# Two whole rows or four half rows: how the last block joins the column groups of TensorE

## The chip, the cores and the metric

The kernel runs on one core of a Trainium2 chip. A core has TensorE (matrix products, result in PSUM), VectorE, ScalarE, GpSimd and SyncE, each with its own list of instructions, and 16 DMA engines that bring data from HBM. The metric is the device time of one execution in microseconds.

## The reference, cut to what matters

```python
B, S, D = 8, 8192, 512                      # x: [B, S, D] fp32, w: [D, D] fp32
mask = (pos < lengths[:, None, None])       # lengths drawn per batch
cs = np.cumsum(x * mask, axis=1)
mid_features = cs[b_idx, lengths // 2, :]   # one row per batch
out = mid_features @ w                      # [8, 512]
```

Only one row of the running sum is used per batch. So what is computed is, for each batch, the sum of its first min(length // 2 + 1, length) rows of x, and then one product with w.

## The kernel before, in words

**Summing with TensorE.** Rows come in blocks of 512: 128 partitions with G = 4 rows each, so a tile of a block is [128, 4, 512]. A matmul with a [128, 8] matrix of ones and zeros as weights adds one of the four rows of all partitions (128 rows of x) to the sums of the 8 batches; the column of the batch that the block belongs to holds ones. A result of 8 rows needs only a quarter of TensorE's columns. The helper `add(j, weights, rows)` (L510 to 515) puts a matmul into column group j: its result stands in partitions 32j to 32j+7 of the PSUM tile s_ps ([128, 512]), and four matmuls with different j can run side by side. Row j of a block goes to group j. At the end the four groups hold four partial sums per batch.

In the profile each fp32 matmul is two records on TensorE (two passes) and two weight loads, which stand under PEld.

**Which blocks there are.** For the lengths drawn, the first full blocks of batches 0 and 1 are in tile first. Another 23 full blocks come through tile xt, in three slots of two blocks each. What is left of each batch, under 512 rows, comes through tile rem. The only full block of the last batch, batch 7, is in tile last: this is the "last block".

**Who issues what.** SyncE issues the transfers of first, xt and last (L188, L222, L255). ScalarE issues those of w and rem. The transfers of last are issued behind all others, in four parts named by ENDS (L63): rows 0 and 1 (512 KB), row 2 (256 KB), the first half of row 3 and its second half (128 KB each). Each part has a semaphore of its own, s_last[0] to s_last[3].

**TensorE's list.** After the first blocks comes a loop over rounds (L555): for each slot it adds up to two blocks and one batch's rest. The order behind the loop is written out by hand:
- L576 to 579: wait for the first part of last, then add its rows 0 and 1 to s_ps, row 0 in group 0 and row 1 in group 1.
- L580, `tell()` (L530): a 1x1 matmul whose end raises s_pe. VectorE waits for it (L496) before it copies s_ps.
- L581 to 586: wait for row 2 and for the first half of row 3, and add them to another PSUM tile, t_ps, with `add_columns(h, weights, row)` (L517). This helper takes half h of the 512 columns and gives 64 columns to each of the four groups. Rows 2 and 3 so bypass s_ps and its copy.
- L587 and 588: wait for VectorE's copy of the first 256 columns of s_ps into s_sb (L498), and fold the four groups' partial sums into t_ps, with a 0/1 matrix (fold) as weights.
- L589 to 593: wait for the second half of row 3, add it to t_ps; wait for the second copy, fold it.
- L594 to 603: the product of the transposed sums (t_sb) with w, 16 matmuls of 128 columns, four groups by four chunks.

**VectorE's list** at that point is two copies of s_ps (256 columns each), two transposes of t_ps into t_sb (L501), and two copies of one half of the result (L506). ScalarE copies the other half (L329). SyncE and ScalarE write one half each (L258, L332). All of VectorE's steps go through the helper `step` (L360).

Of the kernel before, what the change touches and what calls it, by code (L numbers as in the profile page):

```python
# [17 lines left out]
def kernel(  # L18
# [29 lines left out]
    B, S, D = x.shape  # L48
# [25 lines left out]
    def sb(name, shape, dt=F32):  # L74
        return ctx.enter_context(nc.sbuf_tensor(name, shape, dt))

    def ps(name, shape):
        return ctx.enter_context(nc.psum_tensor(name, shape, F32))
# [6 lines left out]
    last = sb("last", [P, G, D])  # L85
# [33 lines left out]
    e_last = sb("e_last", [P, B])  # L119
# [15 lines left out]
    s_ps = ps("s_ps", [P, D])  # L135
# [13 lines left out]
    def take(eng, s, n):  # L149

        eng.wait_ge(s, n).then_inc(s, -n)  # L151

    def pairs(eng, n, body, k=0, most=NS):

        if k < most:
            with eng.If_cmp(n, 2 * k + 1, "IS_GE"):
                body(k)
                pairs(eng, n, body, k + 1, most)

    def rounds_of(eng, n, least):  # L160

        assert all((i + PER - 1) * 43 >> 8 == -(-i // PER) for i in range(ITEMS))
        to = eng.alloc_register(f"{eng.engine.name}_rounds")
        eng.reg_alu(to, n, PER - 1, ALU.add)
        eng.reg_alu(to, to, 43, ALU.mult)
        eng.reg_alu(to, to, 8, ALU.logical_shift_right)
        eng.reg_alu(to, to, least, ALU.max)
        return eng.snap(to, min_val=least, max_val=ROUNDS)

    def less(eng, n, by):  # L170
        eng.reg_alu(n, n, by, ALU.subtract)
        eng.reg_alu(n, n, 0, ALU.max)
# [22 lines left out]
    @contextmanager  # L195
    def ending(eng, name, hint):

        eng.br(name)
        with nc.body(name, valid_engines=OrderedEngineSet([eng.engine])):
            yield  # L200
            eng.br(f"{name}_end").branch_hint(hint)
        nc.switch_bb(f"{name}_end")
# [305 lines left out]

    @block.tensor
    def _(pe):  # L510
        def add(j, weights, rows):

            return pe.matmul(s_ps[32 * j:32 * j + B], lhsT=weights, rhs=rows,  # L513
                             start=False, stop=False, skip_group_check=True,
                             tile_position=(0, 32 * j))

        def add_columns(h, weights, row):  # L517

            for j in range(4):
                at = D // 2 * h + P // 2 * j  # L520
                mm = pe.matmul(t_ps[h][32 * j:32 * j + B, :P // 2], lhsT=weights, rhs=row[:, at:at + P // 2],  # L521
                               start=False, stop=False, skip_group_check=True, tile_position=(0, 32 * j))
            return mm

        def keep_busy(n=1):

            for _ in range(n):
                pe.matmul(idle_ps[:], lhsT=idle[:], rhs=idle[:, :1].to_broadcast((P, D)), start=True, stop=True)  # L528

        def tell():  # L530

            pe.matmul(idle_ps[:1, :1], lhsT=tick[:], rhs=tick[:], start=True,  # L532
                      stop=True).then_inc(s_pe, 1)

        pe.addr_align(256, offset=80, max_nops=0)

        hint = pe.mark_branch_hint_location()
        pe.wait_ge(s_dve, DVE_SEL)
        pe.matmul(s_ps[:], lhsT=zero[:], rhs=zero[:, :1].to_broadcast((1, D)), start=True,  # L539
                  stop=False, skip_group_check=True)  # L540
        pe.wait_ge(s_dve, DVE_N)
        pe.matmul(n_ps[:, :B], lhsT=ones[:], rhs=len_f[:], start=True, stop=True).then_inc(s_pe, 1)  # L542
        pe.wait_ge(s_pool, 2)
        left, some, has_last = [pe.alloc_register(f"pe_{n}") for n in ("left", "some", "has")]
        pe.wait_ge(s_dve, DVE_FIRST)
        pe.load([has_last, left], addr[:, :2])
        pe.reg_mov(some, B)
        rounds = rounds_of(pe, left, RR)
        for b in range(BLIND):
            pe.wait_ge(s_first[b], 16)  # L550
            for j in range(G):
                add(j, cur_first[:, b], first[:, b, j])
        BUSY = [3, 1, 0]
        pe.wait_ge(s_dve, DVE_MASK)
        with pe.Fori(0, rounds):  # L555
            def add_pair(k):
                keep_busy(BUSY[k])
                take(pe, s_full[k], 32)
                with pe.If_cmp(left, 2 * k + 2, "IS_GE"):
                    for j in range(G):  # L560
                        add(j, cur[:, k, 1], xt[:, k, 1, j])
                for j in range(G):
                    mm = add(j, cur[:, k, 0], xt[:, k, 0, j])
                mm.then_inc(s_done[k], 1)

            for k in range(NS):
                pairs(pe, left, add_pair, k, k + 1)
                with pe.If_cmp(some, k + 1, "IS_GE"):
                    take(pe, s_rem[k], 16 * (len(PARTS) + 1))
                    for j in range(G):  # L570
                        mm = add(j, cur_rem[:, k, j * B:(j + 1) * B], rem[:, k, j])
                    mm.then_inc(s_rdone[k], 1)
            less(pe, left, PER)
            less(pe, some, NS)

        with pe.If_cmp(has_last, 1, "IS_GE"):  # L576
            pe.wait_ge(s_last[0], 16)
            for g in range(2):
                add(g, e_last[:], last[:, g])
        tell()  # L580
        with pe.If_cmp(has_last, 1, "IS_GE"):  # L581
            pe.wait_ge(s_last[1], 16)
            for h in range(2):
                add_columns(h, e_last[:], last[:, 2])
            pe.wait_ge(s_last[2], 16)
            add_columns(0, e_last[:], last[:, 3])
        pe.wait_ge(s_dve, DVE_ALL + 1)  # L587
        add_columns(0, fold[:], s_sb[:]).then_inc(s_pe, 1)
        with pe.If_cmp(has_last, 1, "IS_GE"):  # L589
            pe.wait_ge(s_last[3], 16)  # L590
            add_columns(1, e_last[:], last[:, 3])
        pe.wait_ge(s_dve, DVE_ALL + 2)
        add_columns(1, fold[:], s_sb[:]).then_inc(s_pe, 1)
        with ending(pe, "product", hint):  # L594
            pe.wait_ge(s_w, 32)
            for kc in range(KC):
                if kc % 2 == 0:
                    pe.wait_ge(s_dve, DVE_ALL + 3 + kc // 2)
                for j in range(4):
                    mm = pe.matmul(o_ps[32 * j:32 * j + B, :P], lhsT=t_sb[:, kc, :B],  # L600
                                   rhs=wt[:, kc, j * P:(j + 1) * P],
                                   start=(kc == 0), stop=(kc == KC - 1), tile_position=(0, 32 * j))
            mm.then_inc(s_pe, 1)
# [33 lines left out]
```

## Time and profile before

| What | us |
|---|---|
| Time, median of 5 executions | 84.63 (84.38 to 85.02) |
| Time of the profiled execution | 84.69 |
| its span, first to last instruction | 82.9 |
| TensorE busy (385 matmul records) | 56.8 |
| VectorE busy | 15.0 |
| ScalarE busy | 7.4 |
| Landing of the first part of last released TensorE at | 75.80 |
| VectorE's first copy of s_ps started at | 76.89 |
| The output's transfers were issued at | 79.95 and 80.01 |

The span is counted from the first instruction. The time is that of the whole execution, so 1.8 us lie around the span. A view in order of time gives start, length, engine, line, operation, output <- input, shape and number of records; in brackets stands how long the engine was idle before, and what released it. The ends of matmuls are modelled by the profiler, so starts are more telling than lengths: a record of 512 columns shows about 0.59 us, yet the next one in the same group starts 0.43 us after it. The clock granted to TensorE stands per slice in tenths of full speed.

### The profile page before, as it was taken

Reading aid. Unit: us, or ns where it says so; the run is one execution under the profiler, and the core shown is the slowest. Engines: PE = TensorE matmul, PEld = TensorE weight load, DVE = VectorE, ACT = ScalarE, POOL = GpSimd, SP = SyncE. Lnnn points to the kernel's source line nnn. Section 1 sums busy time; section 2 is a strip of 40 time slices with the busy share of each in tenths; the row PEclk is TensorE's granted clock in tenths of the full one; section 3 lists DMA queues with packets and bytes.
Section 4 is the critical chain, followed back from the end, with each engine's and each line's share of the span. In section 5 each row is a group of like instructions: output and inputs, shape, how many; then the busy total and the mean of one; then the engine's idle time right before and its main releaser. Section 6 shows DMA issues by size and latency. Waiting matters only on the chain. (4 is left out here: it accounts for less than half of the span.)

```text
span 82.9 us, 1505 instructions
## 1 busy us (share of the span) xinstructions
PE 56.8 (69%) x385; PEld 15.1 (18%) x385; DVE 15.0 (18%) x79; ACT 7.4 (9%) x8; POOL 1.3 (2%) x14
## 2 busy tenths in 40 slices
PE   2800799297075399999290199999988989188820
PEld 2300023021020112321110011321311411011510
DVE  2858897001001001001000000000000000000620
ACT  0999300000000000000000000000000000000020
POOL 5000000000000000000000000000000000000000
PEclk9999999999999957999999555899999999999999
DMA  0999999999999999999999999999999999997000
GB/s 20 380 419 429 453 427 416 406 419 411 451 435 427 419 387 423 419 407 427 423 427 419 434 432 412 466 411 419 443 411 459 419 411 443 391 400 276 0 1 14
DMA packets 3827, 31.26 MB, mean 377 GB/s; under 512 B 562, under 2 KB 834, under 8 KB 1618
## 3 DMA queue, kind: packets, MB, share of 16 engines
q1 hardware_dynamic: 2754, 27.27, 78.5%
q10 hardware_dynamic: 1072, 3.97, 12.1%
q8 instruction: 1, 0.02, 0.1%
HBM read 31.23 MB, written 0.02 MB: 377 GB/s over the span
## 5 line engine op out<-in xcount | busy, mean ns | idle before, releaser
L513 PE MATMUL s_ps<-xt,cur 128*8 128x512 f32 x184 | 25.0, 663 | 15.6 <-PEq L151 15.6
L528 PE MATMUL idle_ps<-idle 128*128 128x512 f32 x32 | 15.9, 620 | 0.0
L513 PEld LDWEIGHTS s_ps<-xt,cur 128*8 128x8 f32 x184 | 4.2, 92 | 33.7 <-issue 33.7
L477 DVE TENSOR_TENSOR cur<-since 128x16 f32 x9 | 1.7, 188 | 44.4 <-DVEq L151 44.4
L513 PE MATMUL s_ps<-rem,cur_rem 128*8 128x512 f32 x64 | 9.7, 680 | 0.0
L528 PEld LDWEIGHTS idle_ps<-idle 128*128 128x128 f32 x32 | 5.4, 190 | 12.5 <-issue 12.5
L329 ACT COPY o_sb<-o_ps 8x128 f32<-8x128 f32 x2 | 0.5, 259 | 70.4 <-PE o_ps L600 70.4
L513 PE MATMUL s_ps<-first,cur_first 128*8 128x512 f32 x16 | 3.3, 965 | 5.0 <-DVE since L360 5.0
L273 ACT ACTIVATE rem<-rem 128x2048 uint32<-128x2048 uint32 x3 | 5.5, 1892 | 0.0
L513 PEld LDWEIGHTS s_ps<-rem,cur_rem 128*8 128x8 f32 x64 | 2.1, 102 | 6.5 <-issue 6.5
L539 PE MATMUL s_ps<-zero 1*128 1x512 f32 x2 | 2.1, 1136 | 1.6 <-DVE zero L360 1.6
L360 DVE COPY s_sb<-s_ps 128x256 f32<-128x256 f32 x2 | 0.8, 424 | 12.0 <-PE idle_ps L532 11.9
L513 PEld LDWEIGHTS s_ps<-first,cur_first 128*8 128x8 f32 x16 | 0.4, 101 | 6.5 <-issue 5.1
L486 DVE COPY cur_rem<-table 128x32 f32 x5 | 0.9, 181 | 3.4 <-DVEq L151 3.4
L271 ACT ACT_TABLE_LOAD x1 | 1.3, 1283 | 1.9 <-issue 1.9
L600 PE MATMUL o_ps<-wt,t_sb 128*8 128x128 f32 x32 | 1.1, 273 | 0.1
L360 DVE TENSOR_TENSOR part_a<-since,step_a 1x42 f32<-1x42 f32 (+1 forms) x2 | 1.1, 562 | 0.1
L513 PE MATMUL s_ps<-last,e_last 128*8 128x512 f32 x4 | 1.0, 594 | 0.0
L521 PE MATMUL t_ps<-last,e_last 128*8 128x64 f32 x32 | 1.0, 220 | 0.0
L360 DVE TENSOR_TENSOR since<-item,begin 1x42 f32<-1x42 int32 (+1 forms) x2 | 0.8, 422 | 0.1
L600 PEld LDWEIGHTS o_ps<-wt,t_sb 128*8 128x8 f32 x32 | 0.8, 89 | 0.3 <-issue 0.3
L542 PEld LDWEIGHTS n_ps<-len_f,ones 1*128 1x128 f32 x2 | 0.7, 332 | 1.0 <-DVE above L360 0.5
(70 smaller groups left out, 14.2 us busy)
## 6 DMA issues: line engine op xcount, KB each, us to landing
xt<-in_x_dram SPq DMA_DIRECT2D x10, 2048.0 KB, 13.6
xt<-in_x_dram SPq DMA_DIRECT2D x3, 1024.0 KB, 10.9
first<-in_x_dram SPq DMA_DIRECT2D x2, 1024.0 KB, 7.5
rem<-in_x_dram ACTq DMA_DIRECT2D x3, 512.0 KB, 8.0
wt<-in_w_dram ACTq DMA_DIRECT2D x2, 512.0 KB, 5.6
rem<-in_x_dram ACTq DMA_DIRECT2D x3, 256.0 KB, 8.2
last<-in_x_dram SPq DMA_DIRECT2D x1, 512.0 KB, 7.6
rem<-in_x_dram ACTq DMA_DIRECT2D x3, 128.0 KB, 7.8
```

The lines of the kernel that those rows point to most:

```text
L271: act.memzero(lens1[:, 2 * B:])
L273: act.memzero(rem[:, q]).then_inc(s_rfree[q], 1)
L329: copy = act.copy(out=o_sb[1][:, j * P:(j + 1) * P], in_=o_ps[64 + 32 * j:64 + 32 * j + B, :P])
L360: do(*args, **kw).then_inc(s_dve, 1)
L477: dve.tensor_tensor(out=cur[:, k], in0=since[:, :B, here].rearrange("p b h -> p h b"), in1=since[:, 1:, here].rearrange("p b h -> p h b"), ...
L486: dve.tensor_copy(out=cur_rem[:, k], in_=rests[:, ds(dve.snap(of, min_val=1, max_val=RR - 1), 1), k].rearrange("p o w -> p (o w)"),).then_ ...
L513: return pe.matmul(s_ps[32 * j:32 * j + B], lhsT=weights, rhs=rows, start=False, stop=False, skip_group_check=True, tile_position=(0, 32 * j))
L521: mm = pe.matmul(t_ps[h][32 * j:32 * j + B, :P // 2], lhsT=weights, rhs=row[:, at:at + P // 2], start=False, stop=False, skip_group_check= ...
L528: pe.matmul(idle_ps[:], lhsT=idle[:], rhs=idle[:, :1].to_broadcast((P, D)), start=True, stop=True)
L539: pe.matmul(s_ps[:], lhsT=zero[:], rhs=zero[:, :1].to_broadcast((1, D)), start=True, stop=False, skip_group_check=True)
L542: pe.matmul(n_ps[:, :B], lhsT=ones[:], rhs=len_f[:], start=True, stop=True).then_inc(s_pe, 1)
L600: mm = pe.matmul(o_ps[32 * j:32 * j + B, :P], lhsT=t_sb[:, kc, :B], rhs=wt[:, kc, j * P:(j + 1) * P], start=(kc == 0), stop=(kc == KC - 1) ...
```

## The change

`add` takes a slice of columns, which applies to the result and to the moving operand alike. Behind the loop the first part of last is added by four matmuls of 256 columns where there were two of 512: row 0's left half in group 0 and its right half in group 1, row 1's left half in group 2 and its right half in group 3. The folds add all four groups, so it doesn't matter which group a piece of a row is in. All other calls of `add` keep their 512 columns.

```diff
-        def add(j, weights, rows):
-
-            return pe.matmul(s_ps[32 * j:32 * j + B], lhsT=weights, rhs=rows,
+        def add(j, weights, rows, columns=slice(0, D)):
+
+            return pe.matmul(s_ps[32 * j:32 * j + B, columns], lhsT=weights, rhs=rows[:, columns],
                              start=False, stop=False, skip_group_check=True,
                              tile_position=(0, 32 * j))
...
         with pe.If_cmp(has_last, 1, "IS_GE"):
             pe.wait_ge(s_last[0], 16)
-            for g in range(2):
-                add(g, e_last[:], last[:, g])
+            for j in range(4):
+                add(j, e_last[:], last[:, j // 2], slice(D // 2 * (j % 2), D // 2 * (j % 2 + 1)))
         tell()
```

On the engines' lists this is the only difference: two matmuls 8x512 become four of 8x256, and VectorE, ScalarE, GpSimd and SyncE have the same instructions in the same order.

## The prediction

> **What bounds the kernel.** I read the row of slices first, then the chain that ended last, then the tail in order of time.
>
> The slices show two regimes. The granted TensorE clock, the busy share of the DMA engines and the rate, over 40 slices of 2.07 us:
>
> ```profile
> PEclk9999999999999957999999555899999999999999
> DMA  0999999999999999999999999999999999997000
> GB/s 20 380 419 429 453 427 416 406 419 411 451 435 427 419 387 423 419 407 427 423 427 419 434 432 412 466 411 419 443 411 459 419 411 443 391 400 276 0 1 14
> ```
>
> From slice 1 to 35 the DMA engines are full at about 420 GB/s, whatever TensorE does. In slice 36 (74.6 to 76.7 us) they run dry, and what follows no transfer of x bounds. So the body is bound by memory, and the change, which touches no transfer, can only act behind the last landings. The chain that ended last covers just that tail (start us, length, what):
>
> ```profile
> 74.93 1.78 PE s_ps L513 x11
> 76.70 0.06 PE t_ps L521 x3
> 76.77 0.10 PE idle_ps L532
> 76.86 0.02 issue
> 76.89 0.43 DVE s_sb L360
> 77.32 0.02 issue
> 77.34 0.43 DVE s_sb L360
> ...
> 77.87 0.26 DVE t_sb L360
> 78.13 0.14 issue
> 78.27 1.10 PE o_ps L600 x32
> ```
>
> TensorE's last work on s_ps, the 1x1 matmul that tells (L532), two copies of s_ps by VectorE, a transpose, the product. The matmuls on tile last sit ahead of all of it. The tail in order of time shows what released them and what they hold up (start, length, engine, line; idle time and releaser in brackets):
>
> ```profile
> 75.80 0.10 PEld L513 LDWEIGHTS s_ps<-last,e_last 128*8 128x8 f32 x4 [0.76 <-DMA last<-in_x_dram]
> 75.80 1.03 PE L513 MATMUL s_ps<-last,e_last 128*8 128x512 f32 x4
> 76.23 0.08 PEld L532 LDWEIGHTS idle_ps<-tick 128*1 128x1 bf16 x1 [0.33 <-issue]
> 76.47 0.51 PEld L521 LDWEIGHTS t_ps<-last,e_last 128*8 128x8 f32 x23 [0.16 <-issue]
> 76.48 0.28 PE L521 MATMUL t_ps<-last,e_last 128*8 128x64 f32 x4
> 76.66 0.17 PE L532 MATMUL idle_ps<-tick 128*1 128x1 bf16 x1
> 76.67 0.44 PE L521 MATMUL t_ps<-last,e_last 128*8 128x64 f32 x17
> 76.89 0.42 DVE L360 COPY s_sb<-s_ps 128x256 f32<-128x256 f32 x1 [11.93 <-PE idle_ps L532]
> ```
>
> TensorE waits 0.76 us for the landing, then runs four records: each fp32 matmul is two passes, and the two groups run side by side. The first passes start at 75.80, the second at 76.23, and the telling matmul at 76.66, when the streams are through. VectorE, idle for 11.93 us, starts 0.23 us after that. Between landing and copy nothing else decides, so what is saved in these two passes reaches VectorE at once.
>
> **The change, term by term.**
>
> *Removed:* two 512-column matmuls, one in group 0 and one in group 1, that is 4 pass records. Their streams take from 75.80 to 76.66: 0.862 us for two passes in sequence, 0.431 each.
>
> *Added:* four 256-column matmuls, one per group, 8 pass records and 8 weight loads where there were 4. Two passes in sequence again, each half as wide. No row has this width, so I take it between two that are there. The product's 32 records of 128 columns are four groups by eight passes; they take 1.06 us in order of time, less one record of 0.273, over seven spacings: 0.112 each. With 0.431 at 512, the line between them gives 0.112 + 0.319 x 128/384 = 0.218 at 256. Two passes are 0.436, and the saving is 0.862 - 0.436 = **0.43 us**. Halving the 512-column row gives the same 0.43.
>
> Does it cost anything to start in four groups, where two groups ran? The main loop's eight records in four groups start at 74.93 and take 1.04 us in order of time; the four records in two groups take 1.03. So four streams of 512 columns run at the pace of two, and the added starts cost about 0.01. That neighbouring groups read different slices of the same row is how every matmul of L521 works. What no row shows is that groups write different column ranges of s_ps at the same time. From one side it costs nothing, as in the main loop. From the other the groups run two by two, and the saving is 0, or all one after another: 8 x 0.218 = 1.74 us, 0.88 more than now. I take nothing, since the main loop is the same tile, the same four groups and the same data path, with only the column offset equal. A gain beyond 0.43 is excluded while the clock is full, as a pass can't be shorter than its columns.
>
> The trace shows weight loads beside running matmuls of other column groups: the 23 loads of about 88 ns in the rows above would be 2.0 us in a row and take 0.51. "TensorE: Matmul & The Clock Gate" of the Trainium skill, in Part 3 under "What overlaps and what doesn't", speaks against the change: weight loads overlap running matmuls only where the row group differs, and here all four share the rows. By that rule the four added loads would stand in the stream, four times 88 ns, and the saving would fall to 0.08 us (84.55 us); the trace contradicts it, so the sum leaves it out.
>
> *Moved:* the telling matmul from 76.66 to 76.23, the first copy from 76.89 to 76.46, the second from 77.34 to 76.91, its end from 77.77 to 77.34. No instruction of another engine is added or moved in its queue, no DMA is issued earlier or later, and there is no new wait. VectorE has nothing else in that time.
>
> *What is late next.* The rows 2 and 3 of the block, which go past s_ps into t_ps, come with three later landings: issue at 68.65, 69.17 and 69.69 us with 7.8, 7.6 and 7.4 us to landing, so about 76.4, 76.8 and 77.1. They do not move, and on TensorE's list each stands ahead of the next fold.
> - Row 2 starts at 76.47 in the rows above, and with its groups free its 16 records (eight starts of about 0.05 us per pass, four passes deep) are through by 76.7.
> - Row 3, first half, is through about 0.14 us after 76.82: at 76.96. The first fold, released by the first copy's end, moves from 77.36 to 76.93. A start that slips by 0.03 us costs nothing: VectorE is in its second copy until 77.34 and the first transpose waits for that.
> - Row 3, second half, needs the landing at 77.1, about 0.05 us to its first weight load (the first transfer, issued at 68.13 and 7.62 us on its way, released the load at 75.80), and two passes of 0.06: the groups are free by 77.28. The second fold is due at 77.82 - 0.43 = 77.39. This cover is **0.11 us**; a landing later by more takes the excess from the gain. Now it is 0.54.
>
> From there on transpose, product, output copies and the two output transfers follow each other with nothing outside the chain, and w has been on the chip since early in the run. All of it moves by 0.43.
>
> *Sum.* The profiled execution took 84.69 us: a span of 82.9 and 1.8 around it. 84.69 - 0.43 = 84.26. It is 0.06 above the median of the five executions, 84.63, so against the median I forecast 84.63 - 0.43 = **84.20 us**. That is 0.51% less, and 0.5%, about what a measurement of this kernel can tell from no change, is 0.42 us: the forecast sits on the edge.
>
> **The rivals.**
>
> *The next landing takes part of it.* For it: the cover behind the last landing shrinks from 0.54 to 0.11 us. Against it: the distance from the first to the last of the four landings is 512 KB at the rate of the slices, about 1.3 us, and must grow by a tenth before anything is lost. If it grows by 0.3 us, 0.2 is lost: 84.4 us. I give it 0.08.
>
> *The change doesn't do what it says:* the groups write different columns two by two, or the telling matmul waits as long as before. Then nothing is gained: 84.6 us. For it: no row shows the pattern. Against it: the main loop at the pace of one group. 0.06.
>
> *Slower: the code of the tail stalls on its way in.* Two more matmuls are eight more instructions ahead of the whole tail, so every later instruction of TensorE lies eight places further on. If a piece of the program that was there in time must now be fetched between the telling matmul and the product, the chain stands still. The trace has one fetch of instructions inside the span, 16 KB in 0.96 us, at 82.2 us behind everything. One such stall gives 84.63 - 0.43 + 0.96 = 85.16 us. It decides from the point where the stall exceeds 0.43 us and lies ahead of the product. Against it: no stretch of the tail before shows such a hole, and TensorE's gaps there are at most 0.4 us, each with a releaser. 0.07.
>
> *The granted clock falls in the tail,* with less work on TensorE. The stretches of 3.4 us that were followed by half clock had 1.14 and 1.29 us of busy TensorE; one with 1.48 was not. These two show the difference (length, busy, clock, DMA share, GB/s):
>
> ```profile
> 42.36:45.78 3.42, 1.29 (x13) 1.00 0.95 403
> 73.08:76.50 3.42, 2.68 (x26) 1.00 0.91 344
> ```
>
> The tail's stretch would lose about 0.5 us and keep 2.2, far from 1.3. I give it 0.02; it would cost some 0.9 us in the product (eight passes of 0.11) and end at 85.1.
>
> **How the numbers follow.** The forecast has 0.77, the partly taken gain 0.08, no gain 0.06, the stall 0.07, the clock 0.02. The forecast's own 0.77 is split by the edge: the term itself is known to some 0.02 us, but medians of executions that lie between 84.38 and 85.02 scatter by 0.1 to 0.2, so I put 0.51 beyond 0.5% and 0.26 within. With the partly taken and the missing gain (0.08 + 0.06) within 0.5% is 0.40; the stall and the clock make 0.09 slower. The range is from 83.95 (the forecast less a scatter of 0.25) to 84.65, which takes in both cases without gain and leaves out the slower ones.
>
> **What the changed profile would show.** Eight records of 128x256 on s_ps from tile last, in two sets about 0.22 us apart; the telling matmul about 0.43 us after the landing's first start, where it was 0.86; VectorE's copy 0.66 us after that start, where it was 1.09; the last weight loads for row 3 still behind their landing, but the second fold released by the copy. If the sets are 0.43 apart, the groups don't share; if the second fold starts later than 0.04 us after the second copy, the landing or the code holds it. The forecast is wrong if the landings of the four parts drift apart, or if TensorE's code comes late.

## The result and the profile after

The changed kernel took 84.34 us (median of 50 executions, 84.05 to 85.61) against 84.61 us (94 executions) for the kernel before: 0.27 us less. Executions over 1.5% longer than the fastest of their kernel count as disturbed and are left out of every ratio and of the table further down. The ratio is 0.9962 with a 95% interval of 0.9949 to 0.9974, a gain of 0.22 to 0.43 us. The forecast was 84.20, a gain of 0.43. Two later measurements, of 12 executions each, gave 0.999 (0.996 to 1.0019) and 0.9991 (0.9965 to 1.0018). So the first measurement shows a gain, with its middle of 0.38% under the edge of 0.5%, and the two later ones show none that is clear of their noise.

The body is as it was. The rows of slices of the changed kernel, to be held against those in the prediction:

```profile
PEclk9999999999999957999999555799999999999999
DMA  1999999999999999999999999999999999999000
GB/s 18 375 397 429 433 422 428 457 417 393 457 421 405 445 425 381 429 401 433 444 414 421 448 438 412 414 445 437 397 453 429 405 460 405 409 399 339 4 1 6
```

The chain that ended last, of the changed kernel (start us, length, what):

```profile
75.01 1.49 PE s_ps L513 x16
76.50 0.05 PE idle_ps L532
76.56 0.02 issue
76.58 0.43 DVE s_sb L360
...
77.57 0.26 DVE t_sb L360
77.83 0.14 issue
77.96 1.10 PE o_ps L600 x32
```

The steps and their lengths are those of before, but for the first: TensorE's piece on s_ps is 1.49 us, where it was 1.78. The piece on t_ps ahead of the telling matmul (0.06) is gone: row 2 is no longer mixed in with the passes on s_ps. The tail in order of time, of the same execution:

```profile
75.89 0.62 PE L513 MATMUL s_ps<-last,e_last 128*8 128x256 f32 x8
76.11 0.08 PEld L532 LDWEIGHTS idle_ps<-tick 128*1 128x1 bf16 x1
76.32 0.17 PE L532 MATMUL idle_ps<-tick 128*1 128x1 bf16 x1
76.56 0.45 PEld L521 LDWEIGHTS t_ps<-last,e_last 128*8 128x8 f32 x24 [0.36 <-DMA last<-in_x_dram]
76.58 0.88 DVE L360 COPY s_sb<-s_ps 128x256 f32<-128x256 f32 x2 [11.53 <-PE idle_ps L532]
77.06 0.12 PEld L521 LDWEIGHTS t_ps<-s_sb,fold 128*8 128x8 f32 x8
77.21 0.12 PEld L521 LDWEIGHTS t_ps<-last,e_last 128*8 128x8 f32 x8
77.52 0.12 PEld L521 LDWEIGHTS t_ps<-s_sb,fold 128*8 128x8 f32 x8 [0.19 <-DVE s_sb L360]
```

Eight records of 256 columns; the telling matmul starts 0.43 us after them (76.32 - 75.89), where it took 0.86. VectorE's copy starts 0.69 us after the first pass, where it took 1.09: 0.39 us were saved in the chain. This execution received the first part of last 0.09 us later than the profiled execution before (75.84 against 75.75), so its span is shorter by 0.32 only (82.56 against 82.88). TensorE now waits for row 2 (0.36 us, with the DMA as releaser), as the forecast had it: what is late next is a landing. But the second fold (77.52) is still released by VectorE's copy and not by the landing of row 3.

### The profile page after: what moved, and what is told of

The parts are those of the page before. It is cut to its first block, busy times and chain, and to the rows that moved or that the text cites. A ratio compares the mean times of both kernels' runs of the same rounds, so it can differ in the third digit from the quotient of the medians.

```text
span 82.6 us, 1513 instructions
## 1 busy us (share of the span) xinstructions
PE 56.6 (69%) x389; PEld 14.9 (18%) x389; DVE 15.0 (18%) x79; ACT 7.4 (9%) x8; POOL 1.3 (2%) x14
## 5 line engine op out<-in xcount | busy, mean ns | idle before, releaser
L539 PEld LDWEIGHTS s_ps<-zero 1*128 1x128 f32 x2 | 0.5, 304 | 1.6 <-DVE zero L360 1.6
```

## The experiments

Every execution has a time and a span, the latter given to 0.1 us. Their difference is what lies around the span. The table has both, because the answer lies between them.

| Kernel | n | Ratio to before (95%) | Median us | Median span | Around, mean | Around > 2.05 |
|---|---|---|---|---|---|---|
| before, beside the runs below | 92 | | 84.60 | 82.8 | 1.82 | 1 |
| changed, first measurement | 50 | 0.9962 (0.9949 to 0.9974) | 84.34 | 82.4 | 1.96 | 12 |
| e1, e11: changed again | 24 | 0.999, 0.9991 | 84.59, 84.55 | 82.5 | 2.10 | 10 |
| e2: halves in two groups | 11 | 1.0035 (0.9999 to 1.0071) | 84.82 | 82.9 | 1.94 | 3 |
| e3: half the work | 9 | 0.9927 (0.9891 to 0.9963) | 84.20 | 82.4 | 1.85 | 0 |
| e4: all past the sums | 10 | 1.0066 (1.0022 to 1.0109) | 85.31 | 83.4 | 1.92 | 1 |
| e5: changed, code 8 earlier | 12 | 1.0002 (0.998 to 1.0024) | 84.63 | 82.5 | 1.99 | 5 |
| e6: before, code 8 later | 12 | 1.0013 (0.9988 to 1.0038) | 84.50 | 82.7 | 1.83 | 1 |
| e7: e4, code 60 earlier | 6 | 1.0198 (1.0161 to 1.0234) | 86.03 | 84.1 | 2.02 | 3 |
| e8: changed, code 16 later | 6 | 1.0147 (1.0109 to 1.0186) | 85.62 | 83.8 | 1.81 | 0 |
| e9: before, 7 more in front | 12 | 1.006 (1.0032 to 1.0088) | 85.23 | 82.9 | 2.07 | 5 |
| e10: before, 8 more behind | 9 | 0.9989 (0.9963 to 1.0015) | 84.55 | 82.8 | 1.79 | 0 |
| e12: changed, less idle work | 12 | 0.9975 (0.9945 to 1.0005) | 84.41 | 82.3 | 2.01 | 4 |

### Do four groups side by side make the gain? (e1, e2, e3)

e1 is the changed kernel again. e2 has its four matmuls, in two groups. e3 has half of them, in two groups, and leaves out columns 256 to 511 of rows 0 and 1, so its sums are incomplete:

```diff
-            for j in range(4):
-                add(j, e_last[:], last[:, j // 2], slice(...))
+                add(j // 2, e_last[:], last[:, j // 2], slice(...))      # e2
...
+            for j in range(2):                                           # e3
+                add(j, e_last[:], last[:, j], slice(0, D // 2))
```

> The changed kernel once more, beside the others on one chip. Forecast's theory: the first part's two passes take 0.43 us in place of 0.86, VectorE's first copy starts about 0.69 us after the first of these passes (1.09 before), and the time is 0.3 to 0.4 us under the kernel before. Rival, the landing of row 3's second half takes part of the gain: the second fold starts more than 0.05 us after the end of VectorE's second copy.

> The same four matmuls of 256 columns, but row 0's two halves both in group 0 and row 1's in group 1. As many instructions as the changed kernel, no more groups than the kernel before. If the gain comes from four groups side by side: four passes of 0.22 us in sequence, 0.87 us from the first to the telling matmul, and the time of the kernel before (84.6, ratio 1.00). If it comes from narrower matmuls or from where the code lies: 0.3 us faster, like the changed kernel.

> Two matmuls of 256 columns, rows 0 and 1 in groups 0 and 1, columns 0 to 255 alone; columns 256 to 511 of these two rows (of each partition) are left out. Half the streams of the changed kernel in half the groups. If two more groups cost nothing: 0.43 us from the first pass to the telling matmul, and the time of the changed kernel (0.3 to 0.4 us under before). If two more groups and four more records cost something, this one is faster than the changed kernel by it, first of all in the time from the telling matmul to VectorE's copy: 0.23 us as in the kernel before, where the changed kernel has 0.26.

e2, in order of time:

```profile
75.55 1.04 PE L513 MATMUL s_ps<-last,e_last 128*8 128x256 f32 x8
76.42 0.17 PE L532 MATMUL idle_ps<-tick 128*1 128x1 bf16 x1
76.66 0.88 DVE L360 COPY s_sb<-s_ps 128x256 f32<-128x256 f32 x2 [11.95 <-PE idle_ps L532]
```

e3, in order of time:

```profile
75.78 0.60 PE L513 MATMUL s_ps<-last,e_last 128*8 128x256 f32 x4
76.22 0.17 PE L532 MATMUL idle_ps<-tick 128*1 128x1 bf16 x1
76.44 0.88 DVE L360 COPY s_sb<-s_ps 128x256 f32<-128x256 f32 x2 [11.49 <-PE idle_ps L532]
```

With the same eight records in two groups the telling matmul comes 0.87 us after the first pass, and nothing is gained. Half the records in two groups come to 0.435 us, exactly what the changed kernel needs for all of them in four. So the passes gain by the groups alone, the streams side by side cost nothing, and writing different column ranges at the same time is free. Both expectations of the theory came true for the chain. Of the times, e2's shows no gain (84.82); e3's is read by its medians, 84.20 against 84.59 beside it, which is 0.39 us as in the chain, and not by its ratio, which would be 0.62.

One small cost is left, from the telling matmul to the copy: 0.226 us in e3 and in the kernel before, 0.243 in e2, 0.260 in the changed kernel (0.259 in e1). The last group's last pass starts 6 or 7, 13 and 20 ns after the first group's, and the telling matmul starts as soon as the first group is free (in the changed kernel 0.216 us after that group's last pass). So the step grows with the offset of the last group, but by more than the offset itself; what the rest is stays open. It takes 0.034 us of the forecast 0.43.

In e1 the second fold starts 0.05 us after the copy's end, as in the changed kernel and in the kernel before (0.05 each): the landing of row 3's second half takes nothing.

### Where does the rest of the gain go? (e1, e5, e6, e9 to e12)

Between the medians of span 0.3 to 0.4 us are gained in every measurement of the changed kernel. But what lies around the span grew from 1.82 to 1.96 and 2.10 on the mean. It doesn't grow evenly: before, one execution of 92 has over 2.05; the changed kernel has 22 of 74, up to 2.53. The profiled execution of e1 is one of them (84.77 us, span 82.44, around it 2.33). Its trace holds one fetch of instructions of 16 KB, which started 1.22 us after the end of the span and took 1.33 us, while all semaphore records behind the span lie where they lie in an execution with 1.81. In the kernel before a fetch of the same size started 0.65 us ahead of the span's end and took 0.96, and the time around the span was 1.81. That the longer time of e1 is a wait for its fetch was not shown: the fetch ends 2.55 us behind the span, and only 2.33 us lie around the span in all.

What moves this fetch? The first thought was the place of TensorE's program, which has eight instructions more. e5 and e6 shift it by line 535:

```diff
-        pe.addr_align(256, offset=80, max_nops=0)
+        pe.addr_align(256, offset=72, max_nops=0)      # e5, on the changed kernel
+        pe.addr_align(256, offset=88, max_nops=0)      # e6, on the kernel before
```

> The changed kernel with TensorE's program placed eight instructions earlier (the offset of line 535 is 72, not 80), so that everything behind the four matmuls lies where it lay before the change. The span itself should not move (82.4 us). Theory, the place of the code: what lies around the span falls from a mean of 1.95 to 2.1 us back to 1.82, and the time to 84.2, 0.4 us under before (ratio 0.995). Rival, the mere number of instructions or chance: around the span stays at 1.95 or more, ratio 0.997 to 0.999.

> The kernel before, with TensorE's program placed eight instructions later (offset 88), where the changed kernel has its tail. Not one instruction of the tail differs. Theory, the place of the code: the span stays at 82.7 to 82.9 us and what lies around it rises from 1.82 to 1.95 or more, with single executions up to 2.5; the time rises by 0.1 to 0.3 us. Rival: nothing changes, 84.6 us.

Neither theory came true: e5 kept the long times around its span (1.99), e6 stayed at 1.83. The place of the tail doesn't decide. The next thought was the length of the program. e9 puts two idle matmuls of 128x8 (eight records more, but one wait of TensorE's sequencer less: seven instructions, not the eight of the expectation) into TensorE's idle start, with offset 72; e10 puts two behind the product; e12 makes the changed kernel's program as long as that of before:

```diff
+        for _ in range(2):      # e9: behind line 542; e10: behind line 603
+            pe.matmul(idle_ps[:, :B], lhsT=idle[:], rhs=idle[:, :B], start=True, stop=True)
...
-        BUSY = [3, 1, 0]
+        BUSY = [1, 1, 0]        # e12, on the changed kernel
```

> The kernel before with two small idle matmuls (128x8) behind line 542, where TensorE has nothing to do, and its program placed eight instructions earlier (offset 72), so that loop and tail lie where they lay. The tail is that of the kernel before. Theory, the length of TensorE's program sets what lies around the span: span as before (82.7 to 82.9), around it 1.95 or more on the mean, with single executions of 2.2 to 2.5. Rival, it comes with the earlier end of the work: around the span 1.83 as before, time 84.6.

> The kernel before with two small idle matmuls (128x8) behind the product, beside VectorE's output copies; nothing ahead of them moves. Theory, the length of the program or the place of its end: span as before, around it 1.95 or more on the mean. Rival, only the earlier end of the work does it: 1.83 and 84.6 us.

> The changed kernel once more, beside the two above. Span 82.3 to 82.5 in most executions, 0.35 to 0.4 under before; what lies around it scatters from 1.8 to 2.5 where before stays within 1.77 to 2.0. Time between 84.3 and 84.6 us.

> The changed kernel with one idle matmul in place of three ahead of the first slot of each round (BUSY = [1, 1, 0]), so that its program is as long as that of the kernel before. Theory, the length of the program: around the span 1.83 again, and if the clock keeps up, span 82.4 and time 84.2 us, the best of all. Rival 1, the length is not it: around stays at 1.95 or more. Rival 2, with less idle work the clock falls to half more often: longer spans, 83 us or more, clock under 0.9.

e9 is the clearest case: a tail that doesn't differ from that of before (telling matmul 0.86 us after the first pass, copy 0.23 later), a span of 82.9, and yet around it 2.07 on the mean with five executions of 2.3 to 2.54. So the effect needs no earlier end of the work and none of the new matmuls. e10 shows none of it, and e12, as long as before, shows it (2.01). Length alone doesn't decide either. What goes together in the 14 traces, of before, changed and e1 to e12: where a fetch of 16 KB lies within the last 3.2 us of the span (before, e4, e6, e8, e10), the kernel's mean around the span is 1.79 to 1.92; where none lies there (changed, e1, e2, e3, e5, e7, e9, e11, e12), it is 1.85 to 2.14. That holds between kernels and not within their traces: of these nine, e1's alone shows the fetch behind the span, e7's has 1.96 around it, and the other seven have no fetch of 16 KB at all and 1.81, as before. So the fetch goes with the long times without being shown as their cause, and what in the program moves it stays open. e12's median of 84.41 is the lowest of its four, but its interval reaches 1.0005: no version is shown to beat the changed kernel. Its rival of a falling clock shows in the granted clock of its profiled execution (0.897, where e11 has 0.959) and not in its span.

### A shorter tail that was slower (e4, e7), and a fetch in the body (e8)

In e4 rows 0 and 1 also go past s_ps, so the telling matmul doesn't wait for last at all:

```diff
+        tell()
         with pe.If_cmp(has_last, 1, "IS_GE"):
             pe.wait_ge(s_last[0], 16)
             for g in range(2):
-                add(g, e_last[:], last[:, g])
-        tell()
+                for h in range(2):
+                    add_columns(h, e_last[:], last[:, g])
...
         pe.wait_ge(s_dve, DVE_ALL + 1)
-        add_columns(0, fold[:], s_sb[:]).then_inc(s_pe, 1)
+        add_columns(0, fold[:], s_sb[:])
+        with pe.If_cmp(has_last, 1, "IS_GE"):
+            pe.wait_ge(s_last[2], 16)
+            add_columns(0, e_last[:], last[:, 3])
+        tell()
...
```

The second half of the columns is treated alike, with s_last[3]. e7 is e4 with offset 20, e8 the changed kernel with offset 96.

> Rows 0 and 1 go past s_ps into t_ps, like rows 2 and 3, so the telling matmul stands right behind the loop and VectorE's copies don't wait for the last block; each half of row 3 is added behind the fold, and a telling matmul of its own raises the signal for the transpose. If in the changed kernel the chain through the two copies still ends last: the copies are over before the landing of row 3's first half, the first transpose starts about 0.4 us behind that landing (77.25 for 77.57), and the time is about 0.3 us under the changed kernel, 84.0. If the landing of row 3's second half already decides there: no faster than the changed kernel.

> The version in which rows 0 and 1 go past s_ps, with TensorE's program placed 60 instructions earlier (offset 20), so that its end lies where the kernel before has it. Theory, the place of the code: the 0.6 us by which its span was longer, ahead of the last landing, goes away, the tail from the first landing of tile last to the output's copies stays 0.29 us shorter than in the changed kernel, and the time is 84.0 to 84.2. Rival, that version's own instructions are what cost: the span stays at 83.3 us or more and the time at 85.2 or more.

> The changed kernel with its program 16 instructions later (offset 96). Theory, the place of the code: what lies around the span is no better than in the changed kernel (1.95 to 2.1 us), and may grow further. Rival: as the changed kernel with any offset.

e4's VectorE, in order of time:

```profile
77.40 0.88 DVE L360 COPY s_sb<-s_ps 128x256 f32<-128x256 f32 x2 [11.11 <-PE idle_ps L532]
78.48 0.61 DVE L360 STREAM_TRANSPOSE t_sb<-t_ps 128x64 f32<-128x64 f32 x2 [0.20 <-PE idle_ps L532]
80.00 0.60 DVE L360 COPY o_sb<-o_ps 8x128 f32<-8x128 f32 x2 [0.91 <-PE o_ps L603]
```

The tail became as short as expected: from the landing of the first part (77.05) to the output copy (80.00) it takes 2.95 us, where the changed kernel needs 3.24 (75.84 to 79.08). But the landing itself came 1.2 us later, and the time rose by 0.66% over before. e8, the changed kernel with nothing but its program 16 instructions later, lost the same: its first part landed at 77.03, its tail from there to the output copy took 3.25 us as in the changed kernel, and all six of its spans lie between 83.5 and 84.4. What it has around the span fell to 1.81, against its expectation. e7's theory failed too: its tail is short (2.88 us), but the span is 84.1. The third section of the pages (queue, packets, MB, share) gives the lead; e8 has a second fetch, where the page of before has one and that of the changed kernel none:

```profile
q8 instruction: 2, 0.03, 0.2%
```

The trace records put that fetch at 32.1 us in e8 (1.07 us long), at 31.9 in e4 (1.07) and at 2.9 in e7 (1.01), all in the body. And a transfer lands in 16 pieces, one for each DMA engine. The pieces of last's first part, in us:

```
          first   15th    16th   fetch in the body
before    75.02   75.65   75.75  no
changed   75.13   75.51   75.84  no
e5        75.06   75.52   75.63  no
e4        75.08   75.52   77.05  at 31.9
e8        75.14   75.58   77.03  at 32.1
e7        75.25   76.25   77.43  at 2.9
```

In e4 and e8 fifteen of sixteen pieces land as early as ever, and one is late by 1.4 to 1.5 us. In e7 the fetch is earlier, and the last piece is again 1.2 us behind the fifteenth. The landings of the transfers ahead of last show when this begins. In e8 and e4 the last transfer of xt to land before the fetch is late by 0.03 us at most in its last piece; the first one behind the fetch by 1.71 and 1.55, and every later one by 1.4 to 2.2. In e7 the lag is there from the first landings behind its fetch, those of w and first (1.4 to 2.0). Later on it stays with the transfers that SyncE issues: those of rem, issued by ScalarE, lag by 0.46 us at most from 39 us on. This fits a fetch that occupies one DMA engine: that engine's share of SyncE's later transfers is late by it, and each wait is for the slowest of the sixteen, so in a body bound by memory it reaches the end. That the engine which fetched is the one that was late was not seen as such, since the records of landings don't name the engine, and why the lag is 1.4 us and more where the fetch took 1.07 stays open. The moment at which the lag begins and three cases of three speak for it, and in none of the eleven traces without such a fetch is the last piece of last's first part over 0.33 us late. "Runtime: NRT & Kernel Launch" of the Trainium skill, under "Instruction fetch mechanics", says that code comes in blocks of 16 KiB and that crossing into the next one is mostly hidden. The size agrees with these fetches (16384 bytes each); that it is hidden doesn't hold for e4, e7 and e8.

## Why the prediction was right, and what was off

- *Body bound by memory, change acts behind the last landing:* right. The slices show the same full DMA engines (378 GB/s over the span, 377 before), and only the tail differs.
- *A pass of 256 columns takes 0.218 us:* measured 0.219 and 0.216 (telling matmul 0.435 after the first pass; 0.436 was forecast). The line between 128 and 512 columns was good to 2 ns.
- *Four groups cost nothing, other column ranges included:* right, by e2 and e3. The weight loads beside running passes cost nothing either: the eight of the changed kernel don't delay the second passes, which start 0.219 us after the first.
- *The copy follows the telling matmul by 0.23 us as before:* off by 0.034, which grows with the offset between the first and the last group. The chain so gained 0.39 and not 0.43.
- *What is late next:* the cover behind the last landing was worked out as 0.11 us. In the profiled execution the second half of row 3 is through at about 77.35, and the second fold starts at 77.52: 0.17. That rival took nothing.
- *The sum "84.63 - 0.43", worked out from "a span of 82.9 and 1.8 around it":* this is the term that was mis-sized. The 1.8 was carried over as a constant, though no row of the profile shows it. It grew to 1.96 on the mean in the first measurement and to 2.10 in the later ones, and so 0.14 to 0.28 of the chain's 0.39 us were given back outside the span. Why it grew stays open.
- *The range, 83.95 to 84.65:* it takes in the case without any gain too, so that the time lies in it says little. The mechanism is borne out by the chain and by e2 and e3, not by the time.
- *The rival "the code of the tail stalls on its way in":* it did not happen in the changed kernel, but it was the right thing to fear and too narrowly placed. The fetch that goes with the greatest loss in the changed kernel lies in the middle of the body (e8, 16 instructions further on: 1.5% slower than before), ahead of the last landing and not behind it.
- *The rival "the granted clock falls in the tail":* not in the changed kernel's profiled execution, whose clock is full from 52.6 us to the end of the span. In e6's, with the tail of before, it was 0.50 from 72.2 to 75.6 us: TensorE began on last at 76.45, 0.79 us after the landing (75.66), and the span was 83.5 where e6's median is 82.7. Spans of 83.3 to 83.8 stand in 12 of the 92 executions of before too; whether the clock made those isn't shown.

## What to carry to other kernels

Spread the last matmuls in front of a hand-over over all column groups: the time is that of the group with the most columns, and the trace's start-to-start distances give the gain to a few hundredths of a microsecond beforehand. In a program that is bound by its transfers, a shift of a few instructions can go with an instruction fetch in the body that costs more than the change gains; so compare spans and landings, piece by piece, before blaming the instructions that were changed. And a time that lies outside the span is a term of the sum like any other: a gain of 0.4 us is not there until the whole time shows it.

## What the runs showed of the hardware

- A transfer's landing is sixteen landings, and one late piece sets it: 77.03 against 75.58 us for the other fifteen (e8).
- The fetches of instructions of 16 KB took 0.93 to 1.33 us here. With one inside the body, the last piece of SyncE's later transfers landed 1.1 us or more behind the others; one within the last 3.2 us of the span alone (before, e6, e10) went with no such lag; the one seen behind the span came with 0.5 us more around it.
- TensorE starts work for a free column group ahead of an earlier instruction of a busy one: in the kernel before four passes of row 2 start at 76.48, ahead of the telling matmul at 76.66, which stands before them in the program. That the four are those of groups 2 and 3, which had no work from rows 0 and 1, follows from the program; the records don't name the group.
